# Longer rows for some transfers of an add-and-GELU kernel, and stores split by partitions

## The chip, the cores and the metric

The kernel runs on one core of a Trainium2 chip. The time is the device time of one execution in microseconds (us), as a median over several runs. A ratio compares the fast runs of two kernels in the same rounds, so it is not quite the ratio of the medians that stand beside it. A transfer is one instruction that moves data between HBM (the large memory outside the core) and the on-chip memory; its rows are shared out over 16 DMA engines (in the trace of the kernel before, 15 transfers leave 240 completions, 16 each), and one row of one partition is one packet (15 transfers of 128 rows, 1920 packets beside the completions). Times "by the packet records" come from the trace's records of single DMA packets, whose clock starts a few tenths of a us off the profile's; differences between them are good to 0.01 us.

## The reference

```python
# x, y: (1024, 4096) float32
def reference(x, y):
    z = x + y
    return (0.5 * z * (1 + np.tanh(np.sqrt(2 / np.pi) * (z + 0.044715 * z ** 3)))).astype(np.float32)
```

33.55 MB come in, 16.78 MB go out, and there is little arithmetic on them.

## The kernel before

Each of the 128 partitions holds 8 rows of the matrix, that is 32768 columns of float32. x lands in one large tile `z` that is added to, and overwritten with the result, in place. y passes through two buffers of 8192 columns. Work goes in 32 pieces of 1024 columns: GpSimd adds (VectorE for the first piece), ScalarE squares, VectorE multiplies, ScalarE takes the sigmoid, VectorE multiplies again. All transfers are issued from one queue, SyncE's, loads first and stores after.

```python
    YS = 8192
    CH = 1024
    PS = 4
    loads = [2048, 6144, 8192, 8192, 8192]
    stores = [8192, 8192, 8192, 4096, 4096]
    # ...
    def load_x(i):
        a, b = lr[i]
        nc.sync.dma_start(out=zt[:, a:b], in_=xv[:, a:b])

    def load_y(i):
        a, b = lr[i]
        s, o = divmod(a, YS)
        if o == 0:
            yt[s] = pool_y.tile([P, YS], fp32, tag="y", name=f"y{s}")
        nc.sync.dma_start(out=yt[s][:, o : o + b - a], in_=yv[:, a:b])

    def store(i):
        a, b = sr[i]
        nc.sync.dma_start(out=ov[:, a:b], in_=zt[:, a:b])
    # ...
    sp = []
    for i in range(len(loads)):
        sp += [(load_x, i), (load_y, i)]
    sp += [(store, i) for i in range(len(stores))]
    # ... VectorE's order: the multiply of piece i, then the product of piece i - 1
    for i in range(-3, C + 1):
        if 0 <= i < C:
            dve.append((stt, i))
            acts.append((sig, i))
        if 0 <= i - 1 < C:
            dve.append((mul, i - 1))
        # ...
```

Of the kernel before, what the change touches and what calls it, by code (L numbers as in the profile page):

```python
# [1 line left out]

# [1 line left out]

# [4 lines left out]


def begin_early(nc, count):


    blocks = nc.main_func.blocks
    head, body = blocks[0], blocks[1]
    SP = mybir.EngineType.SP
    queue = [i for i in body.instructions if i.engine == SP]
    moved = [i for i in queue if isinstance(i, mybir.InstDMACopy)][:count]
    assert not any(i.sync_info and i.sync_info.on_wait for i in moved)
    at = next(k for k, i in enumerate(head.instructions) if i.engine == SP and isinstance(i, mybir.InstDrain))  # L20
    for k, i in enumerate(moved):
        body.instructions.remove(i)
        head.instructions.insert(at + k, i)


@with_exitstack
def kernel(
    ctx: ExitStack,
    tc: tile.TileContext,
    x: bass.AP,  # L30
    y: bass.AP,
    out: bass.AP,
):








    nc = tc.nc
    P = nc.NUM_PARTITIONS
    fp32 = mybir.dt.float32
    act = mybir.ActivationFunctionType
    alu = mybir.AluOpType

    N, D = x.shape
    assert N % P == 0
    TOT = N // P * D  # L50
    xv, yv, ov = (a.rearrange("(p n) d -> p (n d)", p=P) for a in (x, y, out))

    c1 = 2.0 * math.sqrt(2.0 / math.pi)
    root = math.sqrt(c1 * 0.044715)

    YS = 8192
    CH = 1024
    PS = 4
    loads = [2048, 6144, 8192, 8192, 8192]
    stores = [8192, 8192, 8192, 4096, 4096]  # L60

    def ranges(sizes):
        ends = [sum(sizes[: i + 1]) for i in range(len(sizes))]
        assert ends[-1] == TOT
        return [(e - f, e) for e, f in zip(ends, sizes)]

    lr, sr, cr = ranges(loads), ranges(stores), ranges([CH] * (TOT // CH))
    C = len(cr)
    by_pool = set(range(1, C))

    def over(rs, lo, hi):
        return [i for i, (a, b) in enumerate(rs) if a < hi and b > lo]

    pool_sb = ctx.enter_context(tc.tile_pool(name="xz", bufs=1))
    pool_y = ctx.enter_context(tc.tile_pool(name="y", bufs=2))
    pool_w = ctx.enter_context(
        tc.tile_pool(name="w", bufs=PS, space=bass.MemoryType.PSUM)
    )

    zt = pool_sb.tile([P, TOT], fp32, tag="z", name="z")  # L80
    yt, wt = {}, {}

    def load_x(i):
        a, b = lr[i]
        nc.sync.dma_start(out=zt[:, a:b], in_=xv[:, a:b])  # L85

    def load_y(i):
# [5 lines that stand above are left out]

    def store(i):
        a, b = sr[i]
        nc.sync.dma_start(out=ov[:, a:b], in_=zt[:, a:b])

    def add(c):
        a, b = cr[c]
        s, o = divmod(a, YS)  # L100
        eng = nc.gpsimd if c in by_pool else nc.vector
        eng.tensor_add(out=zt[:, a:b], in0=zt[:, a:b], in1=yt[s][:, o : o + b - a])  # L102

    def sq(c):
        a, b = cr[c]
        wt[c] = pool_w.tile([P, CH], fp32, tag="w", name=f"w{c}")
        nc.scalar.activation(  # L107
            out=wt[c], in_=zt[:, a:b], func=act.Square, scale=root
        )

    def stt(c):
        a, b = cr[c]
        nc.vector.scalar_tensor_tensor(  # L113
            out=wt[c], in0=wt[c], scalar=c1, in1=zt[:, a:b], op0=alu.add, op1=alu.mult
        )

    def sig(c):
        nc.scalar.activation(out=wt[c], in_=wt[c], func=act.Sigmoid)  # L118

    def mul(c):  # L120
        a, b = cr[c]
        nc.vector.tensor_mul(out=zt[:, a:b], in0=wt[c], in1=zt[:, a:b])  # L122


    sp = []
    for i in range(len(loads)):
        sp += [(load_x, i), (load_y, i)]
    sp += [(store, i) for i in range(len(stores))]
    pool = [(add, c) for c in range(C) if c in by_pool]
    dve, acts = [], []  # L130
# [6 lines that stand above are left out]
        if 0 <= i + 3 < C and i + 3 not in by_pool:  # L137
            dve.append((add, i + 3))
        if 0 <= i + 2 < C:
            acts.append((sq, i + 2))  # L140

    needs = {
        load_x: lambda i: [],
        load_y: lambda i: [
            (add, c)
            for c in over(cr, lr[i][0] - 2 * YS, lr[i][0] - YS)
            if lr[i][0] % YS == 0
        ],
        add: lambda c: [(f, i) for i in over(lr, *cr[c]) for f in (load_x, load_y)],
        sq: lambda c: [(add, c)] + ([(mul, c - PS)] if c >= PS else []),  # L150
        stt: lambda c: [(sq, c)],
        sig: lambda c: [(stt, c)],
        mul: lambda c: [(sig, c)],
        store: lambda i: [(mul, c) for c in over(cr, *sr[i])],
    }
    queues = [sp, pool, acts, dve]
    done = set()
    with tc.manual_schedule():
        one = pool_sb.tile([P, 1], fp32, tag="one", name="one")
        nc.vector.memset(one, 0.0)  # L160
        nc.scalar.activation(out=one, in_=one, func=act.Sigmoid)  # L161
        while any(queues):
            moved = False
            for q in queues:
                while q and all(n in done for n in needs[q[0][0]](q[0][1])):
                    fn, arg = q.pop(0)
                    fn(arg)
                    done.add((fn, arg))
                    moved = True
                    if q is not sp:  # L170
                        break
            assert moved, [q[:1] for q in queues]

    ctx.close()
    tc.close()
    tc.compile()
    begin_early(nc, 2)


# [1 line left out]
_INS = ['x', 'y']  # L181
_OUTS = [((1024, 4096), 'float32')]


# [23 lines left out]
```

## Time and profile before

| | before |
|---|---|
| time, us (first 3 runs) | 122.65 (122.49 to 122.69) |
| span of the profiled execution, us | 121.2 |
| busiest compute engine | VectorE, 62% |
| share of the DMA queue | 97.8% |
| bytes by the slope of the packets (435 GB/s), us | 115.7 |

The prediction below shows the lines and reads them. The DMA engines are hardly ever idle between the first packet and the last (by the packet records for 0.31 us at most), and they move some 420 to 440 GB/s in every stretch after the first 5 us.

### The profile page before, as it was taken

Reading aid. Unit: us, or ns where it says so; the run is one execution under the profiler, and the core shown is the slowest. Engines: PE = TensorE matmul, PEld = TensorE weight load, DVE = VectorE, ACT = ScalarE, POOL = GpSimd, SP = SyncE. Lnnn points to the kernel's source line nnn. Section 1 sums busy time; section 2 is a strip of 40 time slices with the busy share of each in tenths; the row PEclk is TensorE's granted clock in tenths of the full one; section 3 lists DMA queues with packets and bytes.
Section 4 is the critical chain, followed back from the end, with each engine's and each line's share of the span. In section 5 each row is a group of like instructions: output and inputs, shape, how many; then the busy total and the mean of one; then the engine's idle time right before and its main releaser. Section 6 shows DMA issues by size and latency. Waiting matters only on the chain.

```text
span 121.2 us, 248 instructions
## 1 busy us (share of the span) xinstructions
DVE 75.5 (62%) x66; ACT 63.8 (53%) x66; POOL 73.0 (60%) x35
## 2 busy tenths in 40 slices
DVE  0044700059999019999997999994999999400000
ACT  4016200078875047888858878874878878000000
POOL 0056000699980299999889999949999990000000
DMA  6999999999999989898989898998999999989992
GB/s 197 417 468 422 471 406 433 476 389 476 389 476 389 476 379 487 357 508 357 508 346 519 346 519 346 346 487 381 479 389 476 389 476 389 487 379 411 433 433 108
DMA packets 2162, 50.35 MB, mean 416 GB/s; under 512 B 240, under 2 KB 240, under 8 KB 240
## 3 DMA queue, kind: packets, MB, share of 16 engines
q1 hardware_dynamic: 2160, 50.33, 97.8%
q14 instruction: 2, 0.02, 0.0%
HBM read 33.55 MB, written 16.78 MB: 415 GB/s over the span
## 4 chain that ended last, share of the span: by engine, by line
DMA 49%; POOL 17%; DVE 16%; SPq 1%; ACT 1%; issue 0%; POOLq 0%
DMA y<-in_y_dram 49%; POOL z L102 17%; DVE z L122 8%; DVE w L113 8%; ACT w L107 1%; SPq L85 1%; SPq L92 1%; POOLq L102 0%
## 5 line engine op out<-in xcount | busy, mean ns | idle before, releaser
L102 POOL TENSOR_TENSOR z<-z,y 128x1024 f32<-128x1024 f32 x31 | 72.8, 2388 | 26.5 <-DMA y<-in_y_dram 26.5
L113 DVE SCALAR_TENSOR_TENSOR w<-w,z 128x1024 f32<-128x1024 f32 x32 | 39.4, 1232 | 21.4 <-ACT w L107 21.4
L107 ACT ACTIVATE w<-z 128x1024 f32<-128x1024 f32 x32 | 32.9, 1028 | 37.7 <-POOL z L102 31.7
L122 DVE TENSOR_TENSOR z<-w,z 128x1024 f32<-128x1024 f32 x32 | 38.8, 1214 | 0.0
L118 ACT ACTIVATE w<-w 128x1024 f32<-128x1024 f32 x32 | 31.4, 981 | 0.4 <-DVE w L113 0.4
L102 DVE TENSOR_TENSOR z<-z,y 128x1024 f32<-128x1024 f32 x1 | 1.2, 1224 | 6.1 <-DMA y<-in_y_dram 6.1
L161 ACT ACT_TABLE_LOAD x1 | 1.3, 1283 | 1.3 <-PEq L192 1.3
L160 DVE MEMSET one<- 128x1 f32 x1 | 0.1, 59 | 1.3 <-PEq L192 1.3
L192 POOL MEMSET const-float32-0.0<- 128x1 f32 x1 | 0.1, 99 | 0.2 <-issue 0.2
L161 ACT ACTIVATE one<-one 128x1 f32<-128x1 f32 x1 | 0.2, 203 | 0.0
L192 POOL MEMSET const-bfloat16-1.0<- 128x1 bf16 x1 | 0.1, 102 | 0.0
L192 POOL MEMSET const-uint8-127<- 128x1 uint8 x1 | 0.1, 102 | 0.0
L192 POOL MEMSET const-float32-1.0<- 128x1 f32 x1 | 0.1, 99 | 0.0
## 6 DMA issues: line engine op xcount, KB each, us to landing
z<-in_x_dram SPq DMA_DIRECT2D x3, 4096.0 KB, 34.2
y<-in_y_dram SPq DMA_DIRECT2D x3, 4096.0 KB, 24.8
out_dram<-z SPq DMA_DIRECT2D x3, 4096.0 KB, 30.8
out_dram<-z SPq DMA_DIRECT2D x2, 2048.0 KB, 17.5
z<-in_x_dram SPq DMA_DIRECT2D x1, 3072.0 KB, 13.4
y<-in_y_dram SPq DMA_DIRECT2D x1, 3072.0 KB, 20.4
z<-in_x_dram SPq DMA_DIRECT2D x1, 1024.0 KB, 4.9
y<-in_y_dram SPq DMA_DIRECT2D x1, 1024.0 KB, 6.9
```

The costliest lines, as they stand in the source:

```text
L85: nc.sync.dma_start(out=zt[:, a:b], in_=xv[:, a:b])
L92: nc.sync.dma_start(out=yt[s][:, o : o + b - a], in_=yv[:, a:b])
L102: eng.tensor_add(out=zt[:, a:b], in0=zt[:, a:b], in1=yt[s][:, o : o + b - a])
L107: nc.scalar.activation(out=wt[c], in_=zt[:, a:b], func=act.Square, scale=root)
L113: nc.vector.scalar_tensor_tensor(out=wt[c], in0=wt[c], scalar=c1, in1=zt[:, a:b], op0=alu.add, op1=alu.mult)
L118: nc.scalar.activation(out=wt[c], in_=wt[c], func=act.Sigmoid)
L122: nc.vector.tensor_mul(out=zt[:, a:b], in0=wt[c], in1=zt[:, a:b])
L160: nc.vector.memset(one, 0.0)
L161: nc.scalar.activation(out=one, in_=one, func=act.Sigmoid)
L192: nc = _bacc.Bacc("TRN2", target_bir_lowering=False, num_devices=1)
```

## The change

Its intent is fewer, longer packets: the last two loads of x become one with rows of 64 KB, and so do the first two stores. The other three stores are each split in two halves, partitions 0 to 63 and 64 to 127, which keeps their rows long and brings the number of transfers to 16.

```diff
-    loads = [2048, 6144, 8192, 8192, 8192]
-    stores = [8192, 8192, 8192, 4096, 4096]
+    loads_x = [2048, 6144, 8192, 16384]
+    loads_y = [2048, 6144, 8192, 8192, 8192]
+    stores = [16384, 8192, 4096, 4096]
 ...
     def store(i):
         a, b = sr[i]
-        nc.sync.dma_start(out=ov[:, a:b], in_=zt[:, a:b])
+        cut = [0, 64, P] if i > 0 else [0, P]
+        for f, e in zip(cut, cut[1:]):
+            nc.sync.dma_start(out=ov[f:e, a:b], in_=zt[f:e, a:b])
 ...
-    for i in range(len(loads)):
-        sp += [(load_x, i), (load_y, i)]
+    for i, (a, b) in enumerate(lr):
+        sp += [(load_x, k) for k, r in enumerate(xr) if r[0] == a] + [(load_y, i)]
```

(The rest of the diff gives x its own list of ranges.)

## The prediction

In full the sum was 122.65 - 0.06 = 122.6 us if the split costs nothing (A), and 122.6 + 19.4 = 142.0 us at half rate (B). The 19.4 us of B is the time of step (4) once more: at half rate, and with the second half after the first, 38.8 us for 19.4.

> **What bounds the kernel now.** I read the page's list of busy engines first, to see whether a compute engine fills the span; then the slices, to see whether transfers do; then the share of the DMA queue.
>
> ```profile
> DVE 75.5 (62%) x66; ACT 63.8 (53%) x66; POOL 73.0 (60%) x35
> ...
> DMA  6999999999999989898989898998999999989992
> ...
> q1 hardware_dynamic: 2160, 50.33, 97.8%
> ```
>
> No compute engine is over 62% busy, while the 16 DMA engines are busy 97.8% of the 121.2 us, from the second slice to the last but one. The kernel moves 50.33 MB (16.78 MB each of x, y and out), and nothing in it can end before those bytes have moved. The chain of waits starts from the last compute instruction and so ends at 104.3 us; it does not show the last stores. To see what the end hangs on I look at the windows of the stages and at the timeline of the issuing queue.
>
> ```profile
> core 0: us, DVE busy (x) ACT busy (x) POOL busy (x), PEclk, DMA share, GB/s
> ...
> 61.00:81.00 20.00, 19.07 (x18) 16.10 (x18) 18.50 (x8) 1.00 1.01 419
> 81.00:101.00 20.00, 18.32 (x17) 15.35 (x17) 18.50 (x8) 1.00 1.01 435
> 101.00:122.00 21.00, 3.32 (x3) 1.68 (x2) 0.00 (x0) 1.00 0.84 360
> ```
>
> ```profile
> 36.05 0.33 SPq L92 DMA_DIRECT2D y<-in_y_dram  x1
> ...
> 60.08 0.33 SPq L92 DMA_DIRECT2D y<-in_y_dram  x1
> ...
> 60.52 44.17 SPq L96 DMA_DIRECT2D out_dram<-z  x5
> ...
> 104.35 0.33 SPq L96 DMA_DIRECT2D out_dram<-z  x1
> ```
>
> From 81 to 101 us only stores run, at 435 GB/s. The last store is issued at 104.35 us while some 16 us of earlier stores are still queued, so compute has 10 us or more to spare at the end. All loads lie before all stores in one queue.
>
> The trace's records of single DMA packets (no view prints them, so I give the numbers) show how near the queue is to its best. A row of 8, 16, 24 or 32 KB is one packet of mostly 309, 611, 912 or 1213 ns, and the next packet of that engine starts about 4 ns before the end of the last. The slope is (1213 - 309) / 24 KB = 37.7 ns per KB, which is 27.2 GB/s for one engine and 435 for 16. What is left beside the slope is 309 - 4 - 301 = 4 ns a packet. At the slope alone the bytes need 50.33 MB / 435 GB/s = 115.7 us. The rest of the span is 1.1 us to the first packet, 0.7 us of slow first packets, 0.8 us in one slow packet on each engine near 77 us (its last row but one of the loads), 120 rows an engine of 4 ns = 0.5 us, small slow-downs and one engine that runs 0.4 us late, and 1.2 us from the last landing to the end. The change can win only from this.
>
> [...] in the trace before, every transfer has 128 rows and 16 completions[...] no transfer in it covers half the partitions. What it shows is the full rate of 435 GB/s for stores over all 128.
>
> **The change part by part.** The instructions of the four compute engines are the same in number and in order; only the transfers change.
>
> (1) x columns 16384 to 32767 come in one transfer of 64 KB rows, and so does out for columns 0 to 16383. Each takes 8 packets off each engine: 16 x 4 ns = 0.06 us less. One transfer more in all (16 for 15) adds one completion packet of 5 ns an engine. Sum: -0.06 us.
>
> (2) The loads change order: the queue is x0 y0 x1 y1 x2 y2, then 8 MB of x, then y3, y4. Before it was x3 y3 x4 y4. So y3 lands when x4 did, by the packets at 70.4 us and not at 60.7. Nothing is idle in the queue: y3 is issued at about 36 and y4 at about 60.1, when their buffers are free, as before, and the 8 MB of x keep the queue full until 60.7. But the third quarter of the adds now starts at about 70.6 us. The group of GpSimd adds takes 18.52 us for 8, or 2.315 each; 16 adds run without a gap to 70.6 + 16 x 2.315 = 107.6 us (before: 99.7). Behind its last add the chain before needs 104.3 - 99.7 = 4.6 us for square, multiply, sigmoid and product. The last product so ends at 112.2 us and not 104.3.
>
> (3) Is that still hidden? By the completions before, the queue has done everything but the last 2 MB at 114.1 (first engine) to 115.0 us (last). The stores of the last 4096 columns are issued at about 112.3, and from the first issue to the first packet the trace shows 1.1 us: 113.4. That is 0.7 us ahead of need. The earlier ones are easier: columns to 24575 are done at 70.6 + 8 x 2.315 + 4.6 = 93.7 and needed at 99.6; those to 28671 at 103.0 and needed at 109.2; the 8 MB store at 63.5 and needed at 80. So it costs 0, with a margin that is only just there.
>
> (4) The last 8.39 MB of stores go as two halves of 64 partitions. Each engine has the same rows and bytes, 8 x 32 KB + 16 x 16 KB, and each is full-length, so by engine rate it takes 8 x 1.209 + 16 x 0.607 = 19.4 us as before. [...]
>
> [...]
>
> **The rivals.** A: [...] 122.6 us. For it speaks [...] that someone who has tuned to single microseconds, with an early issue of two transfers, split the stores on purpose. I have no number for that. B: half rate; 142 us. [...] C: between, when [...] neighbours drift apart and mix the halves: at three quarters of the rate 19.4 / 3 = 6.5 us more, 129. D: the last product is late: when the last stores are issued 1 or 2 us later than worked out, the queue runs dry for as long, and the time is 123 to 124.5. It is small and would come on top of A; under B or C the queue is later and it vanishes. E: the stretch near 77 us costs more with a 64 KB row ahead: at most another 0.8 us. F: 64 KB rows are cut in two by the hardware: the 0.06 us is not even won.
>
> **Range and chances.** Faster by 2% needs 120.2 us, and so most of the start, the slow stretch and the tail gone, which nothing here touches: 3%. Between A (with D, E and F inside it) and B or C I can't decide from a trace that has no half transfer; I give A 55% and the slower ones 42%. The point is A's, 122.6. The distribution has two peaks, so a range for 8 in 10 must span them: 121.8 to 142.3.
>
> **What would show it.** Right or wrong by step: (1) 1920 packets on the queue (1664 rows and 256 completions; before 1920 rows and 240), and the same 50.33 MB; 64 KB packets of 1213 x 2 = about 2.42 us. (2) GpSimd idle for some 10 us before its 16th add, until 70.5, then 16 adds without a gap to 107.6. (3) The last store issued at about 112.3; no empty slice in the DMA row between there and the end. (4) is the one that decides: after about 99.6 us the GB/s row stays near 435 (A) or falls to about 218 (B), and 32 KB packets of stores take 1.21 us or 2.42. The prediction is wrong if that row shows a half or partial rate, or if a gap stands ahead of the last stores; the range is wrong if the time is below 121.8 or over 142.3.

## More of the kernel before

One view is added here to set against the changed kernel: windows of the last stretch of the kernel before. A packet counts whole in the window in which it starts, so a busy share can pass 1. The columns are the window, its length, the busy time (and instructions) of VectorE, ScalarE and GpSimd, the TensorE clock, the busy share of the DMA engines and the GB/s that they moved.

```profile
102.00:112.00 10.00, 2.32 (x3) 1.01 (x1) 0.00 (x0) 1.00 1.01 434
112.00:118.00 6.00, 0.00 (x0) 0.00 (x0) 0.00 (x0) 1.00 1.00 429
118.00:124.00 6.00, 0.00 (x0) 0.00 (x0) 0.00 (x0) 1.00 0.15 66
```

Here stores alone are left, and a busy share of 1 means 429 to 434 GB/s.

## The result, and the profile after

| | before | changed |
|---|---|---|
| time, us (6 runs each) | 122.67 (122.49 to 123.08) | 135.37 (135.03 to 135.66) |
| ratio, 95% interval | | 1.1032 (1.1007 to 1.1056) |
| span, us | 121.2 | 133.6 |
| share of the DMA queue | 97.8% | 96.5% |

The changed kernel is slower by 12.7 us. First the page of its profile: busy engines, the DMA row of the slices with the rate under it, and the share of the queue.

```profile
DVE 75.5 (57%) x66; ACT 63.8 (48%) x66; POOL 73.0 (55%) x35
...
DMA  6999999999899779797999797997969799699970
GB/s 216 461 422 464 419 412 432 471 471 422 363 471 628 314 314 628 314 442 343 471 471 442 343 628 314 473 473 314 589 226 285 157 236 245 177 265 304 353 270 34
...
q1 hardware_dynamic: 1920, 50.33, 96.5%
```

The busy times of the compute engines are those of before to 0.1 us, and there are 1920 packets as worked out. The DMA engines are nearly as busy as before, too: no slice before the last has less than 6 tenths, and by the packet records, counted by overlap, the engines are busy 1.00 of the time from 102 to 124 us, so nothing waits for an issue. But the rate falls to about a half from the 30th slice on (97 to 100 us), within which the split stores begin. (A packet counts in the slice where it starts, so single slices jump, above all with 64 KB rows.) The windows of the last stretch say it more plainly:

```profile
102.00:112.00 10.00, 10.00 (x9) 7.47 (x8) 5.58 (x3) 1.00 1.04 229
112.00:118.00 6.00, 0.21 (x1) 0.00 (x0) 0.00 (x0) 1.00 0.86 213
118.00:124.00 6.00, 0.00 (x0) 0.00 (x0) 0.00 (x0) 1.00 0.97 281
124.00:134.00 10.00, 0.00 (x0) 0.00 (x0) 0.00 (x0) 1.00 0.56 205
```

From 102 to 112 us the DMA share is 1.04, and the rate is 229 GB/s where it was 434. So the busy share doesn't show whether an engine moves data at full rate or is held up within its packets; here only the rate beside it does. Further on, with 16 KB rows, the rate rises to 281.

The compute side came as predicted. From the chain of waits and the timeline of the changed kernel (start, length, what):

```profile
70.60 2.35 POOL z L106
...
109.91 2.30 DVE z L126 x2
```

```profile
76.42 38.95 SPq L100 DMA_DIRECT2D out_dram<-z  x7
```

The third quarter of the adds starts at 70.60 us, and the last product ends at 112.21. The stores are issued from 76.42 us on, while loads are still in flight.

By the packet records, from the last engine's completion of the 8 MB store to that of the two 32 KB halves 18.0 us pass, and from there to the end of the four 16 KB halves 14.6. A whole store of the same bytes takes 9.7 us (8 packets of 1.209 us). So the 32 KB halves lose 8.3 us and the 16 KB halves 4.9. A 32 KB packet of the first halves takes 2.55 us in the median where it took 1.21.

### The profile page after: what moved, and what is told of

Its sections match the earlier page's. It is cut to its first block, busy times and chain, and to the rows that moved or that the text cites. A ratio compares the mean times of both kernels' runs of the same rounds, so it can differ in the third digit from the quotient of the medians.

```text
span 133.6 us, 244 instructions
## 1 busy us (share of the span) xinstructions
DVE 75.5 (57%) x66; ACT 63.8 (48%) x66; POOL 73.0 (55%) x35
## 3 DMA queue, kind: packets, MB, share of 16 engines
q1 hardware_dynamic: 1920, 50.33, 96.5%
## 4 chain that ended last, share of the span: by engine, by line
DMA 41%; DVE 29%; POOL 12%; ACT 1%; issue 0%; SPq 0%; POOLq 0%
DMA y<-in_y_dram 41%; DVE z L126 14%; DVE w L117 14%; POOL z L106 12%; ACT w L111 1%; SPq L87 0%; POOLq L106 0%
## 5 line engine op out<-in xcount | busy, mean ns | idle before, releaser
L126 DVE TENSOR_TENSOR z<-w,z 128x1024 f32<-128x1024 f32 x32 | 38.8, 1215 | 0.0
```

Source lines behind the costliest of these rows:

```text
L126: nc.vector.tensor_mul(out=zt[:, a:b], in0=wt[c], in1=zt[:, a:b])
```

## The experiments

Theory P: a store that reads only partitions 0 to 63, or only 64 to 127, of the on-chip memory runs at about half rate, as the windows above have it (229 and 213 GB/s for 434 and 429). Its rivals: the 64 KB rows and the later loads are to blame (R); the number of transfers (N); the writing to HBM, or any transfer of 64 rows (H). Twelve kernels ran, each against the kernel before on the same chip. A table first; all are correct except the fourth.

| run | what | time, us (range) | before | ratio (95%) |
|---|---|---|---|---|
| e1_rows_only | the change without its split | 122.45 (122.35 to 122.64) | 122.89 | 0.9971 (0.9955 to 0.9987) |
| e2_split_only | before, with the split alone | 136.0 (134.94 to 136.84) | 122.89 | 1.1047 (1.0971 to 1.1122) |
| e3_columns | split by columns in its place | 122.22 (122.01 to 123.05) | 122.89 | 0.9963 (0.9927 to 1.0) |
| e4_shifted | halves read partitions 32 to 95 | 122.22 (122.0 to 122.53) | 122.89 | 0.9953 (0.9932 to 0.9974) |
| e5_first_only | only 32 KB rows split | 132.13 (131.72 to 132.38) | 122.73 | 1.076 (1.0731 to 1.0789) |
| e6_last_only | only 16 KB rows split | 128.08 (128.01 to 128.32) | 122.73 | 1.0443 (1.0427 to 1.0459) |
| e7_loads | before, last loads split | 142.62 (142.55 to 142.75) | 122.73 | 1.1626 (1.1609 to 1.1644) |
| e9_sixteen_rows | one store in eight parts | 137.79 (136.12 to 138.94) | 122.73 | 1.1186 (1.1109 to 1.1262) |
| e8_short_rows | all split rows 16 KB | 130.38 (130.08 to 131.28) | 122.84 | 1.0634 (1.0592 to 1.0676) |
| e10_half_ahead | and 8 engines put behind | 130.65 (129.34 to 132.23) | 122.84 | 1.0644 (1.0594 to 1.0693) |
| e11_all_behind | and all 16 put behind | 131.55 (131.12 to 131.92) | 122.84 | 1.0716 (1.0683 to 1.0748) |
| e12_shorter_rows | all split rows 8 KB | 123.53 (123.42 to 123.65) | 122.84 | 1.0064 (1.0047 to 1.0081) |

The longest run of e9_sixteen_rows and that of e10_half_ahead were slow and are not in the ratios; they are in the ranges and medians.

### Which part of the change costs it

e1_rows_only, against the changed kernel:

```diff
-        cut = [0, 64, P] if i > 0 else [0, P]
+        cut = [0, P]
```

> The changed kernel with its stores not split: 64 KB rows and 13 transfers. Theory P (a store of partitions 0 to 63 or 64 to 127 [...] runs at half rate): the split was all of the loss, so 122.2 to 122.8 us. Rival R (the 64 KB rows, the later landing of y or the later last product cost it): near 135 us. A mixture would lie between.

Measured: 122.45 us. R falls: without the split, the longer rows and the later loads cost nothing, and win 0.3%. This version is 13 us under the changed kernel and 0.3% under the kernel before; e3_columns does as well.

e2_split_only, against the kernel before:

```diff
-        nc.sync.dma_start(out=ov[:, a:b], in_=zt[:, a:b])
+        cut = [0, 64, P] if i > 1 else [0, P]
+        for f, e in zip(cut, cut[1:]):
+            nc.sync.dma_start(out=ov[f:e, a:b], in_=zt[f:e, a:b])
```

> The kernel before with only its last three stores split into halves of 64 partitions, rows of 32 KB as before. P: the same loss as in the changed kernel, +12.7 us, so 134 to 137 us. R: 122.7 us. Rival N (the number of transfers or of completions): more transfers than the change has (18 for 16), so more than 135 if this were the cause.

Measured: 136.0 us, the same loss (13.1 us by the medians), and within P's range. The split alone is enough. N is not excluded by this run, since N expected more than 135 too.

e3_columns, against the changed kernel:

```diff
-        cut = [0, 64, P] if i > 0 else [0, P]
+        cut = [a, (a + b) // 2, b] if i > 0 else [a, b]
         for f, e in zip(cut, cut[1:]):
-            nc.sync.dma_start(out=ov[f:e, a:b], in_=zt[f:e, a:b])
+            nc.sync.dma_start(out=ov[:, f:e], in_=zt[:, f:e])
```

> The changed kernel with each of the last three stores split in two by columns, not by partitions: 16 transfers, the same bytes in each as in the change, all over 128 partitions, rows half as long. P: full rate, 122.2 to 122.9 us. N (16 smaller transfers are dear): near 135 us.

Measured: 122.22 us, with 16 transfers of the bytes that the change has. N falls, and so does the idea that the rows must stay long: 8 and 16 KB rows over 128 partitions run at 425 to 426 GB/s.

### Is it the partitions that are read

e4_shifted, against the changed kernel (its result is wrong):

```diff
         for f, e in zip(cut, cut[1:]):
-            nc.sync.dma_start(out=ov[f:e, a:b], in_=zt[f:e, a:b])
+            g, h = (32, 96) if i > 0 else (f, e)
+            nc.sync.dma_start(out=ov[f:e, a:b], in_=zt[g:h, a:b])
```

> Wrong result on purpose. The changed kernel, but both halves of each split store read partitions 32 to 95 on the chip; the places written in HBM, the sizes, the number and the order of the transfers are those of the change. [...] P: full rate, 122.2 to 122.9 us, packets of 32 KB rows of stores 1.21 us. Rival H (it is the writes to HBM, 64 rows of it at a time, or any transfer of 64 rows, that are slow): 135 us and packets of 2.5 us, as in the change.

Measured: 122.22 us. Windows of e4_shifted for the stretch in which the changed kernel moved 229 and 213 GB/s:

```profile
102.00:112.00 10.00, 9.90 (x9) 7.16 (x8) 5.28 (x3) 1.00 0.97 418
112.00:118.00 6.00, 0.00 (x0) 0.00 (x0) 0.00 (x0) 1.00 1.00 426
```

Nothing differs from the changed kernel but the partitions that are read, and the loss is gone; its 32 KB packets of stores take 1.21 us. H falls: transfers of 64 rows, to the same places in HBM, run at full rate. What matters is which 64 partitions. That these 64 run at full rate (418 and 426 GB/s) is what the run shows, and for other ranges it shows nothing.

e9_sixteen_rows, against the changed kernel:

```diff
-        cut = [0, 64, P] if i > 0 else [0, P]
+        cut = list(range(0, P + 1, 16)) if i == 1 else [0, P]
```

> The changed kernel with its store of 8192 columns split in eight transfers of 16 partitions and the other stores whole. [...] clearly slower than the halves (131). Rival: any split costs one factor of two, whatever its size: 131 us.

Measured: 137.79 us, clearly slower than the halves of the same store (132.13). The expectation's own figure, 151 us, with its ground, a quarter of the rate, was too high. By the packet records the first row of each engine takes 3.76 us in the median and up to 4.49, not the 1.21 of a whole store and not the 2.55 of a half. So with 16 partitions a row takes longer than with 64. But that is only so at first. The last engine ends the 8 parts 24.8 us after the 8 MB store, which is more than the 20.0 of the two halves in e5_first_only, but less than 8 rows of 3.76 us would be, 30.1. A part is only one row for each engine, so engines that are a row apart are at different parts, and so at different partitions. The first and the last engine end the parts 6.2 us apart, and are still 5.2 apart at the end of the whole stores behind, so the end waits for the last engine.

e7_loads, against the kernel before; the same was done to the load of y:

```diff
     def load_x(i):
         a, b = lr[i]
-        nc.sync.dma_start(out=zt[:, a:b], in_=xv[:, a:b])
+        cut = [0, 64, P] if i > 3 else [0, P]
+        for f, e in zip(cut, cut[1:]):
+            nc.sync.dma_start(out=zt[f:e, a:b], in_=xv[f:e, a:b])
```

> The kernel before with its stores whole and the last load of x and of y (8192 columns each, 32 KB rows, 8.39 MB together) split by partitions. If writing into the on-chip memory has the same limit [...] as reading from it: two such pairs at close to half rate, +14 to +19 us, 137 to 142 us. If only reading has it: 122.7 us.

Measured: 142.62 us, +19.9 by the medians, just above the expected range. Windows of e7_loads, one before the split loads, two within them and one in the stores behind:

```profile
42.00:58.00 16.00, 13.09 (x12) 11.94 (x13) 16.00 (x8) 1.00 1.00 432
62.00:78.00 16.00, 14.60 (x14) 12.01 (x13) 16.00 (x8) 1.00 1.05 219
82.00:98.00 16.00, 1.37 (x2) 0.00 (x0) 0.00 (x0) 1.00 1.04 214
102.00:118.00 16.00, 13.15 (x12) 11.99 (x13) 16.00 (x8) 1.00 1.01 434
```

So writing has the limit as well as reading, and here it is a half all through: 8.39 MB at 435 GB/s are 19.3 us, and +19.9 is that once more, with a little on top. The same bytes split in stores lose only 13. That is the next question.

### Why split stores lose less than half

e5_first_only and e6_last_only, against the changed kernel:

```diff
-        cut = [0, 64, P] if i > 0 else [0, P]
+        cut = [0, 64, P] if i == 1 else [0, P]    # e5_first_only
+        cut = [0, 64, P] if i > 1 else [0, P]     # e6_last_only
```

> The changed kernel with only the first of its three split stores still split (8192 columns, 32 KB rows); the two of 4096 columns go over 128 partitions. In the changed kernel these two halves took 117.8 - 99.6 = 18.2 us by their last completions, where a whole transfer takes 9.7, so +8.5 on the 122.45 us without a split: 131.0 us (130 to 132) if the losses of the transfers simply add.

> The changed kernel with only the two stores of 4096 columns split (16 KB rows). In the changed kernel they took 132.4 - 117.8 = 14.6 us for 9.7, +4.9. Theory S (short rows let the two halves mix [...]): 127.4 us, as there. Theory D (the engines have to be pushed out of step first, which in the change the 32 KB halves did): more here, up to half rate all through, +9.7, 132 us.

Measured: 132.13 us, a loss of 9.7 us on e1_rows_only by the medians, and 128.08, a loss of 5.6 (the chips differ; their kernels before differ by 0.2 us). Both are about 1 us above what was expected, and together they lose 15.3 us where the change loses 12.9, so the parts don't simply add. (The expectation's 18.2 us took completions in order of time; sorted by transfer it is 18.0.) In e6_last_only the four 16 KB halves took 15.7 us, in the change, behind the 32 KB halves, 14.6. So S is nearly right and D's start, that something must first push the engines apart, counts for 1 us: short rows lose less by themselves. But why?

The packet records, sorted by transfer, show how far apart the first and the last engine complete each. This is a table of mine from the records, in us, from the whole 8 MB store on (in e7_loads the four halves of the loads, after the y load ahead of them):

```
                    whole   halves, one after the other
changed             0.99    0.85 1.76 (32 KB)  2.72 3.69 4.63 5.34 (16 KB)
e6_last_only        0.98    0.64 1.28 1.83 2.65
e8_short_rows       0.97    0.52 1.16 1.96 2.80 3.49 4.13 4.58 4.72
e12_shorter_rows    0.99    0.90 1.42 1.76 1.78 1.79 1.82 1.83 1.87 ... 2.02
e7_loads            0.98    0.81 0.84 1.75 1.11
```

(In e6_last_only a whole store of 32 KB rows, with 0.98 too, stands between.) In split stores the engines part from half to half, and while they part, the rate recovers: in e6_last_only, by the packet records counted by overlap, about 240 GB/s from 112 to 116 us, then 270, then 280. In the loads of e7_loads they don't part, and the rate stays a half. The author's reading, which no run shows directly: engines that are one half-transfer apart read different halves, and so don't meet in the same 64 partitions. One half-transfer is 4 rows an engine, by the packets at full rate 4 x 1.209 = 4.84 us with 32 KB rows, 2.43 with 16 KB, 1.22 with 8 KB. Theory D now reads: stores of short rows lose less because the engines need to part less far, down to where they are nearly far enough apart to begin with.

e8_short_rows and e12_shorter_rows, against the changed kernel:

```diff
-    stores = [16384, 8192, 4096, 4096]
+    stores = [16384, 4096, 4096, 4096, 4096]     # e8_short_rows
+    stores = [16384] + [2048] * 8                # e12_shorter_rows
```

> The changed kernel with all its split stores in pieces of 4096 columns (16 KB rows, eight halves, 18 transfers). Theory D: the halves stop sharing once the engines [...] are one half-transfer apart, and with 16 KB rows that is 2.43 us in place of 4.85, reached sooner than with 32 KB rows. Four such halves from step took 15.8 us for 9.7 in the run with only the last stores split, so eight take 26 to 31.6 for 19.4: +7 to +12, 129 to 134.5 us, less than the change's 135.4. Rival: row size plays no part, 135.4.

> The changed kernel with all its split stores in pieces of 2048 columns (8 KB rows, 16 halves, 26 transfers). One half-transfer is now 1.22 us, near the 0.9 us by which the engines are apart anyway. D: fewer in step, still less than short rows: 124 to 130 us. Rival: shorter rows don't help, 135, or the number of transfers costs more.

Measured: 130.38 us and 123.53. e12_shorter_rows even does a little better than its range of 124 to 130. All of these windows are of split stores only, first e8_short_rows:

```profile
102.00:112.00 10.00, 9.92 (x9) 7.17 (x8) 5.29 (x3) 1.00 0.98 259
112.00:118.00 6.00, 0.00 (x0) 0.00 (x0) 0.00 (x0) 1.00 0.99 314
118.00:124.00 6.00, 0.00 (x0) 0.00 (x0) 0.00 (x0) 1.00 0.98 377
```

and e12_shorter_rows:

```profile
102.00:112.00 10.00, 9.96 (x9) 7.22 (x8) 5.33 (x3) 1.00 1.01 414
112.00:118.00 6.00, 0.00 (x0) 0.00 (x0) 0.00 (x0) 1.00 1.01 423
118.00:124.00 6.00, 0.00 (x0) 0.00 (x0) 0.00 (x0) 1.00 0.22 90
```

With 16 KB rows the rate climbs from transfer to transfer; with 8 KB rows it is nearly full soon after the start. This fits the table: with 8 KB rows the distance passes one half-transfer (1.22 us) in the second half and then hardly grows, while the rate is 414 and more. With 16 KB rows it passes 2.43 us only in the fourth half, and stops growing at 4.7. The fit is in order and in size, and that short rows recover sooner is shown; that it is the distance that does it is argued from the two going together, not tested apart from each other. The table also gives the distance over all 16 engines and not that between any two of them, for the records don't name the engine.

One rival to the limit on 64 partitions fits e4_shifted as well: that an engine is slow at partitions other than those that it has in a whole transfer. The record speaks against it. The halves of e12_shorter_rows have the same 64 rows, 4 for each engine, as those of the change, and run at 414 to 423 GB/s where those of the change ran at 229 and 213.

e10_half_ahead and e11_all_behind tried to make this distance on purpose, against e8_short_rows:

```diff
+    def pad(i):
+        spare = pool_sb.tile([P, 4000], fp32, tag="spare", name="spare")
+        nc.sync.dma_start(out=spare[:8, :], in_=xv[:8, :4000])      # e11_all_behind: 16 rows
 ...
+    sp += [(pad, 0)]
     sp += [(store, i) for i in range(len(stores))]
```

> The kernel with short rows plus one useless load of 8 rows of 16 KB into spare memory, queued between the last load and the first store. [...] Theory D [...] from then on the one half is read by 8 engines while the other 8 read the other half: nearly full rate, 122.4 + 2.4 = 124.8 us, so an added transfer makes it 4 to 9 us faster than the run with short rows alone. If it isn't the phase [...]: as short rows alone, plus 0 to 2.4 us.

> Control for the run before: the same useless load with 16 rows, so that all 16 engines get one and fall behind alike [...]. D: no phase is made, so as short rows alone plus about 2.4 us. If an extra load by itself helped: as fast as the run with 8 rows.

Measured: 129.34 to 131.1 us in the three fast runs and 131.12 to 131.92 in the control, beside 130.08 to 131.28 without a load. The run is not clearly different from that without a load, and far from the 124.8 that was expected. The fast runs lie 1.3 us under the control on average, but with the slow (132.23) only 0.8. The two runs are inconclusive on D, and the records say how. (The trace shows 8 packets and 8 completions of this load, but not which engines they were on; that it would put them 2.4 us behind was not shown.) The packets of the useless load took 0.60 to 1.30 us, not the 2.4 expected. Still, the distance was there: at the end of the whole store the engines were 3.54 us apart (0.97 without the load, 1.35 in the control). But the next half closed it to 1.61. The first completion of that half came 4.57 us after the first of the whole store, near the 4.84 of half rate, and the last 2.65 us after the last, near the 2.43 of full rate: the engines ahead were held back. Which partitions the engines ahead and those behind were at, and so whether they met in the same half, the records don't show; the phase theory has no test of its own.

It also stays open why stores drift apart while loads stay in step. Every packet of the split loads of e7_loads from 64 to 96 us took 2.26 us or more, while of the 16 KB packets of e6_last_only in its first 8 us of halves some took 0.61 us and others 1.5. So at one time the packets of the split stores took unequal times, and those of the split loads didn't. That is a description and not a cause.

## Why the prediction was right or wrong

**Right.** The time lies in the range, but that says little: the range runs from A to past B, and 135.37 lies at neither of its two peaks. What was right is more than that. The deciding step, (4), was named as such, with the sign that would show it: the rate after 99.6 us, and packets of 1.21 or 2.42 us (2.55 was measured). B's half rate is what the split loads of e7_loads show all through (219 and 214 GB/s for 432), and e4_shifted (418 and 426 GB/s) that it hangs on which 64 partitions a store reads. Step (2) came to the tenth: the adds start at 70.60 us (70.6 predicted), the last product ends at 112.21 (112.2). In step (3) nothing ran dry; rival D, the late last product, and E, a dearer stretch near 77 us, are not seen in e1_rows_only. Count and length of the packets in step (1) are right: 1920, and 2.418 us for 64 KB.

**Wrong: the point of 122.6 us.** It was A's, that the split costs nothing, and A fell: the split alone costs 13.1 us (e2_split_only). What is left of A's support in the prediction is that someone who tunes to single microseconds had split the stores on purpose, for which the prediction itself says it has no number. The intent behind a change is no measurement and should not have set the point.

**Mis-sized: the +19.4 us of step (4) under B.** Measured for the split: 32.6 us from the whole store's last completion to the end in the changed kernel, less 19.3 in e1_rows_only, is 13.3. The premise that failed is that the second half doesn't run beside the first. The engines are not held to each other: in the changed kernel the first engine completes the fourth 16 KB half at 127.4 us, the last engine the third only at 129.6 (times of the semaphores). Loads did stay in step and lost the whole 19.9 us; stores drifted, and the shorter the rows, the sooner. C had this in words ("neighbours drift apart and mix the halves") and guessed 6.5 us for it.

**Mis-sized: the 0.06 us of step (1).** e1_rows_only is 0.44 us faster by the medians. What gives the rest is not settled. In the profiled execution of before, packets from 75.5 to 79.5 us are 0.80 us too long in sum for each engine, and 0.40 in e1_rows_only; but in e3_columns and e8_short_rows, with the same long rows, it is 0.80 and 0.90, so this stretch differs between executions. In the kernel before the 0.80 us is one slow packet on each engine, two packets before the stores begin; in the other traces with whole loads the packets there are 0.05 to 1.2 us too long in sum, and where it is little most engines have no slow one. A packet of at least one engine is 0.35 us late or more between 84 and 88 us in all of these traces, which in most of them widens the distance between the first and the last engine to about 1 us. The cause of neither was tested.

**A slip in step (3) that had no effect.** The 8 MB store was said to be ready at 63.5 us; it was issued at 76.42. Its last product, that of piece 15, comes on VectorE behind the multiply of piece 16, and piece 16 now waits for y until 70.5. By the packet records the engines ended the loads at 79.3 to 80.1 us, so the margin was 3 to 4 us and not 16. To say when a result is ready one must look at what stands before it in its engine's own order. Another slip is in the reading of the kernel before: the "some 16 us of earlier stores" at 104.35 us take in the last store itself; by the packet records the earlier ones end at 115.0, 10.7 us on. Step (3) used the right figure.

## What to carry to other kernels

Split a transfer by columns rather than by partitions, and if 64 partitions must do, take 32 to 95, which ran at full rate here (418 and 426 GB/s in e4_shifted), not 0 to 63 and then 64 to 127 (229 and 213 in the changed kernel). Read the rate beside the busy share: the DMA engines showed 96.5% busy with half of the late rate gone. When a changed order makes one piece late, follow every engine's own order from that piece, for it can hold back a result that doesn't depend on it.
